# Retention of a head pair, four tiles at a time, in a hybrid attention, convolution and retention layer

## The chip, the cores and the metric

The kernel runs on one core of a Trainium2 chip. The metric is the device time of one execution in microseconds (us), as the median of several runs. In the rows PE is TensorE (matrix products and transposes), PEld its loading of the stationary operand, DVE is VectorE, ACT is ScalarE, POOL is GpSimd and SP issues the transfers.

## The reference

One layer over 2048 tokens of width 1024. The normalised input goes through one projection whose columns feed three mixers: chunked softmax attention (6 heads of 64), a convolution module, and retention (6 heads of 64). Their outputs meet in one output projection with a residual; a squared-ReLU feed-forward of width 4096 and a gated embedding follow. The part that matters here is the retention, cut to its core:

```python
intra = einsum(einsum(qc, kc) * d_intra, vc)          # inside a chunk, with decay
kv    = einsum(k_dec, vc)                             # 64 x 64 per chunk and head
prev  = scan: state = chunk_decay * state + kv        # state before each chunk
cross = einsum(q_dec, prev)
out   = intra + cross
out   = (out - mean) * rsqrt(var + EPS) * gn_g        # per head
return silu(g) * out
```

## The kernel before, in words

Tokens are worked on in four blocks of 512 (`T`), each of four tiles of 128 tokens (`NT`). A block goes through the projections, mixers, output projection, feed-forward and gate. Large products are done as three fp32r matmuls (high and low parts); transposes and the small products of attention and retention are plain fp32, and the trace shows such a small product as two instructions.

Heads are taken in three pairs. For each pair `att_proj` (L371) and `ret_proj` (L508) make the projections; `ret_proj` leaves per tile a buffer `rn` of 512 columns: q, k (both rotated), v and the gate. The copies out of PSUM for a tile end in two POOL additions and multiplications (L535 finishes q and k, L540 the gate). `rn` tiles come from a pool of four.

`ret_mix` (L546) does the retention of a pair tile by tile, in a loop over the four tiles. Each tile has one PSUM bank `s` from `rbank` (L110), a pool of a single bank, so the next tile's first transpose needs the release of this tile's bank. In the bank the loop puts the transposes of q and k, the scores of both heads, the key-value product and the output. Between the PE steps ACT copies k (L557) and q (L561), DVE writes q once more into `qz` with zeros in the other head's rows (L560), DVE multiplies the scores by the decay mask (L566), ACT copies the output (L575), DVE updates the running state of both heads (L578), and a group norm follows: statistics (L582, L583), epsilon (L585), power -0.5 on POOL (`rstd`, L181 and L182), subtraction of the mean on DVE (L589), two POOL multiplications (L591, L592). After the last tile four transposes (`roT`) bring the output into the layout of the output projection, and `split_tr` (L184) writes its high and low parts.

The order of PE's instructions is written out: every matmul and transpose keeps its program order. `trunk` walks through the large products as segments; after each of their matmuls `advance` (L801) may insert steps of two chains that run beside them, chain 0 the attention of a pair (`att_mix`, L401), chain 1 the retention and the convolution's end (`conv_mix`, L325). A step is a generator's stretch between two `yield`s. The value that is yielded (from the table `W`, L234) is how long PE is to do other work before the chain's next step, measured on a model clock `clk` that grows with each PE instruction by a fixed cost (L48 to L56):

```python
if t[1] > pos and clk[0] < t[4]:   # L816: not yet, unless past its deadline
    break
...
t[4] = clk[0] + d + 0.01           # L822: earliest clock of the next step
```

Retention of pair 0 and 1 may start at a fifth of the next `att_proj`, that of pair 2 at 3% of the output projection's first part (`wo_a`), and has its deadline near the end of the next `ret_proj`, or at the start of `wo_b`. The order on the other engines is the scheduler's.

Of the kernel before, what the change touches and what calls it, by code (L numbers as in the profile page):

```python
# [12 lines left out]
F32R = mybir.dt.float32r  # L13
AF = mybir.ActivationFunctionType
ALU = mybir.AluOpType
AX = mybir.AxisListType

P = 128
D = 1024
S = 2048  # L20
T = 512
NB = S // T
NT = T // P
KT = D // P
HD = 64
# [15 lines left out]
def trunk(ctx, tc, a, out):  # L41
    nc = tc.nc
    V, A, G = nc.vector, nc.scalar, nc.gpsimd
    clk, posn = [0.0], [0.0]

    class PE:
        @staticmethod
        def matmul(o, x, y, start, stop):  # L48
            n = y.shape[-1]
            clk[0] += max(n, 256) / 2400.0 if y.dtype == F32R else max(4 * n, 512) / 2400.0  # L50
            tc.keep_in_program_order(nc.tensor.matmul(o, x, y, start=start, stop=stop))  # L51

        @staticmethod
        def transpose(o, x, i):
            clk[0] += 256 / 2400.0
            tc.keep_in_program_order(nc.tensor.transpose(o, x, i))  # L56

    cpool = ctx.enter_context(tc.tile_pool(name="const", bufs=1))
# [3 lines left out]
    def ctile(name, shape, src=None, dt=F32):  # L62
        t = cpool.tile(shape, dt, tag=name, name=name)
        if src is not None:
            nc.sync.dma_start(t, src)
        return t

    def stile(tag, bufs, shape, name=None, dt=F32):
        return sp.tile(list(shape), dt, tag=tag, name=name or tag, bufs=bufs)
# [40 lines left out]
    def rbank(name):  # L110
        return ps.tile([P, 512], F32, tag="r", name=name, bufs=1)
# [4 lines left out]
    def f(t):  # L116
        return t.bitcast(F32)
# [63 lines left out]
    def rstd(o, var, n):  # L181
        G.tensor_tensor(o, var, nhalf[:, :n], ALU.pow)  # L182

    def split_tr(b, hi, lo, scale):  # L184
        A.activation(hi, b, AF.Copy, scale=scale)
        V.scalar_tensor_tensor(lo, b, scale, f(hi), ALU.mult, ALU.subtract)
# [44 lines left out]
        A.activation(r, b[:, :T], AF.Copy)  # L231

    cur = {}
    W = dict(qk=0.7, qs=2.5, st=5.2, ss=1.2, ts=2.4, vo=1.6, r1=2.6, r2=1.6, r3=1.5, r4=4, c1=3.5, c2=2.6, c3=0.6)  # L234

    def xnorm(blk):
        xh, xl = big("xh", 0), big("xl", 1)
# [87 lines left out]
    def conv_mix():  # L325
# [3 lines left out]
        for u in range(2):  # L329
# [13 lines left out]
            for i in range(2):  # L343
                V.tensor_scalar(z[u][:, i * DC : i * DC + DC], b2[:, i], s6[:, 12 + 2 * i : 13 + 2 * i],
                                s6[:, 18 + i : 19 + i], ALU.subtract, ALU.mult)
            yield W["c1"]
        hl = []
        for c in range(2):
# [7 lines left out]
            hl.append((yh, yl))  # L356
            yield W["c2"]
        yield W["c3"]
        for c in range(2):
# [8 lines left out]
            V.scalar_tensor_tensor(ml[:, c], b, bias, f(mh[:, c]), ALU.add, ALU.subtract)  # L368
            yield W["c2"]

# [25 lines left out]
    def mix():  # L396
        if "m" not in cur:
            cur["m"] = big("mh", 2), big("ml", 3)
        return cur["m"]

    def att_mix(p):  # L401
# [6 lines left out]
        for j, gain in enumerate((qg, kg)):  # L408
# [3 lines left out]
            for h in range(2):  # L412
# [5 lines left out]
                if j == 0:  # L418
                    A.activation(q[h][y], b[x], AF.Copy, scale=gain[x, 0:1])
            yield W["qk"]  # L420
        yield W["qs"]
        rs = stile("rs", 2, [P, 16])
# [121 lines left out]
        yield from gemm(range(NT), KT, 5, tok(xh, xl), lambda t, k: rhs(k), 512, evac)  # L544

    def ret_mix(p):  # L546
        nats = cur["rn", p]
        o = stile("ro", 1, [P, NT, P])
        for t in range(NT):
            n = nats[t]  # L550
            s = rbank("rs")
            for j in range(2):
                PE.transpose(s[:, j * P : j * P + P], n[:, j * P : j * P + P], ident)
            kT = stile("rk", 1, [P, P])
            at = stile("rat", 1, [P, 256])
            qT = stile("rq", 1, [P, P])
            A.activation(kT, s[:, P:256], AF.Copy)  # L557
            for h in range(2):
                hr = slice(h * HD, h * HD + HD)
                V.tensor_copy(qz[hr, h], s[hr, :P])  # L560
            A.activation(qT, s[:, :P], AF.Copy)  # L561
            yield W["r1"]
            PE.matmul(s[:, 256:], kT, qz.rearrange("p h n -> p (h n)"), start=True, stop=True)
            yield 0
            PE.matmul(s[:, P:256], n[:, P : 2 * P], n[:, 256:384], start=True, stop=True)
            V.tensor_tensor(at, s[:, 256:], rmask[:, 2 * p : 2 * p + 2].rearrange("p h n -> p (h n)"), ALU.mult)  # L566
            yield W["r2"]
            PE.matmul(s[:, :P], qT, st[p], start=True, stop=False)
            yield 0
            for h in range(2):  # L570
                hr = slice(h * HD, h * HD + HD)
                PE.matmul(s[:, hr], at[:, h * P : h * P + P], n[:, 256 + h * HD : 256 + h * HD + HD],
                          start=False, stop=(h == 1))
                yield 0
            A.activation(o[:, t], s[:, :P], AF.Copy)  # L575
            for h in range(2):
                hr = slice(h * HD, h * HD + HD)
                V.scalar_tensor_tensor(st[p][hr, hr], st[p][hr, hr], gstate[hr, p : p + 1],  # L578
                                       s[hr, P + h * HD : P + h * HD + HD], ALU.mult, ALU.add)
            g6 = stile("g6", 2, [P, 20])  # L580
            for h in range(2):
                V.bn_stats(g6[:, 6 * h : 6 * h + 6], o[:, t, h * HD : h * HD + HD])  # L582
                V.bn_aggr(g6[:, 12 + 2 * h : 14 + 2 * h], g6[:, 6 * h : 6 * h + 6])  # L583
            gv = g6[:, 12:16].rearrange("p (h c) -> p h c", c=2)[:, :, 1]
            V.tensor_tensor(g6[:, 16:18], gv, geps[:, 2 * p : 2 * p + 2], ALU.add)  # L585
            rstd(g6[:, 18:20], g6[:, 16:18], 2)
            for h in range(2):
                hr = slice(h * HD, h * HD + HD)
                V.tensor_scalar(o[:, t, hr], o[:, t, hr], g6[:, 12 + 2 * h : 13 + 2 * h], None, ALU.subtract)  # L589
            o3 = o[:, t].rearrange("p (h d) -> p h d", d=HD)  # L590
            G.tensor_tensor(o3, o3, g6[:, 18:20].unsqueeze(2).to_broadcast([P, 2, HD]), ALU.mult)  # L591
            G.tensor_tensor(o[:, t], o[:, t], n[:, 384:], ALU.mult)  # L592
            yield W["r3"]
        yield W["r4"]
        mh, ml = mix()
        b = rbank("roT")
        for t in range(NT):
            PE.transpose(b[:, t * P : t * P + P], o[:, t], ident)
        split_tr(b, mh[:, RT[p]], ml[:, RT[p]], gng[:, p : p + 1])
        yield 0  # L600

# [133 lines left out]
    segs, start = [], {}  # L735
# [46 lines left out]
    for b in range(NB):  # L782
        if b:
            place(lambda b=b: xnorm(b), spread(13, at(("g2", b - 1, 6), 0.05), at(("g2", b - 1, 7), 0.95)))
            place(late, spread(8, at(("conv", b), 0.01), at(("conv", b), LE)))
            place(lambda b=b: ple_load(b - 1), [at(("conv", b), 0.3)])
            place(late_rstd, [at(("conv", b), LF), at(("conv", b), LF + 0.15)])
        if b:
            chain(1, conv_mix, at(("ap", b, 0), CS), at(("ap", b, 1), CE))
        for p in range(NPAIR):  # L790
            nxt = ("rp", b, p + 1) if p < 2 else ("wob", b)
            chain(0, lambda p=p: att_mix(p), at(("rp", b, p), AS if b or p else AS0), at(nxt, 0.0))
            chain(1, lambda p=p: ret_mix(p), at(("ap", b, p + 1), RS) if p < 2 else at(("woa", b), RT0),
                  at(nxt, RE if p < 2 else 0.0))
            if b == 0 and p == 0:
                chain(1, conv_mix, at(("ap", b, 1), CS0), at(("rp", b, 2), CE0))
        place(norm2, [at(("g1", b, 0), NE), at(("g1", b, 0), NF)])
# [26 lines left out]
                    c.pop(0)  # L824

    with tc.high_priority(offset=AHEAD):
        nhalf = ctile("nhalf", [P, 4])
        G.memset(nhalf, -0.5)
        ng = ctile("ng", [P, 3, KT])
        ident = ctile("ident", [P, P])  # L830
        make_identity(nc, ident)
        ones = ctile("ones", [P, 1])
        A.activation(ones, nhalf[:, 0:1], AF.Copy, scale=-2.0)
        kdec = ctile("kdec", [P, NH], a["kdec"])
# [5 lines left out]
    for c in range(2):  # L840
        with tc.high_priority(offset=AHEAD):
            next(first)
        x = slice(c * HALF, c * HALF + HALF)
# [18 lines left out]
    rmask = ctile("rmask", [P, NH, P], a["rmask"])  # L862
    geps = ctile("geps", [P, NH], a["geps"])
    gstate = ctile("gstate", [P, NPAIR], a["gstate"])
    hist = ctile("hist", [P, 2, NTAP - 1])
    G.memset(hist, 0.0)
    qz = ctile("qz", [P, 2, P])
    G.memset(qz, 0.0)
    st = []
    for p in range(NPAIR):  # L870
        st.append(ctile(f"st{p}", [P, P]))
        G.memset(st[p], 0.0)

    pos = 0.0
    for gen in segs:
# [92 lines left out]
```

## Time and profile before

| | |
|---|---|
| Median of three runs | 2852.79 us (2850.76 to 2854.25) |
| Span of the profiled execution | 2853.1 us, 0.3 us over the median of the runs |
| PE busy | 2777.3 us, 97% |
| DVE, ACT, POOL busy | 1580.2, 1126.5, 1121.1 us (55%, 39%, 39%) |
| Retention per execution | 12 times `ret_mix` (4 blocks, 3 pairs), 48 tiles |

The page's shares are averages over stages. The timeline gives for a group of instructions its start, its length, and in brackets how long its engine was idle before it and what ended that. The groups by line and shape give busy time, the mean length of one, and the idle time before with its causes. Start to start of neighbouring matmuls is what one costs PE, since their lengths overlap.

### The profile page before, as it was taken

The page shows a single profiled execution, that of the slowest core. Times are in us where ns is not written, and L with a number is a line of the kernel's source. Part 1 is how long each engine was busy: PE and PEld are TensorE (multiplying, and loading weights), DVE is VectorE, ACT ScalarE, POOL GpSimd, SP SyncE. Part 2 cuts the span into 40 slices and gives each one's busy share as a digit, 9 for nine tenths or more (in the row PEclk, how much of TensorE's full clock was granted, in tenths as well). Part 3 has the DMA queues.
Part 4 walks back from the last instruction along what each step waited for, and adds up shares of the span by engine and source line. Part 5 has one row for each costly group of instructions (what it writes and reads, how often), then busy time and mean ns, then how long its engine had stood idle before and what let it go on. Part 6 is the DMA issues. An engine that isn't in the chain of part 4 may idle for free. (4 is left out here: it accounts for less than half of the span.)

```text
span 2853.1 us, 36805 instructions
## 1 busy us (share of the span) xinstructions
PE 2777.3 (97%) x13178; PEld 2233.5 (78%) x13178; DVE 1580.2 (55%) x2811; ACT 1126.5 (39%) x2210; POOL 1121.1 (39%) x1038
## 2 busy tenths in 40 slices
PE   7999999999999999999999999999999999999999
PEld 6777788887788778888778877888877877788887
DVE  6966433348766653334876664333487666433343
ACT  4554322243455432224345543222434554322333
POOL 4434433335444343333544434333354443433333
PEclk9999999999999999999999999999999999999999
DMA  5123222242212322224221232222422122222221
GB/s 179 62 85 115 94 90 95 96 140 88 85 62 75 123 96 90 96 96 138 90 85 62 74 124 96 90 95 96 140 87 85 62 97 82 89 93 93 96 103 67
DMA packets 89030, 271.80 MB, mean 95 GB/s; under 512 B 11024, under 2 KB 11792, under 8 KB 88848
## 3 DMA queue, kind: packets, MB, share of 16 engines
q1 hardware_dynamic: 88848, 269.45, 27.4%
q8 instruction: 105, 1.72, 0.2%
q14 instruction: 77, 0.63, 0.1%
HBM read 261.02 MB, written 8.39 MB: 94 GB/s over the span
## 5 line engine op out<-in xcount | busy, mean ns | idle before, releaser
L123 POOL TENSOR_TENSOR w<-raw,w 128x512 fp32r<-128x512 f32 (+1 forms) x439 | 584.4, 1333 | 1163.8 <-ACT w L122 826.7
L122 ACT ACTIVATE w<-raw 128x512 fp32r<-128x512 f32 (+1 forms) x880 | 536.5, 618 | 1109.5 <-PE acc L51 630.6
L51 PE MATMUL acc<-xh,w 128*128 128x512 f32 (+1 forms) x1744 | 563.9, 396 | 0.0
L51 PE MATMUL acc<-w,xh 128*128 128x512 f32 (+1 forms) x1536 | 489.8, 384 | 3.1 <-DVE w L123 1.9
L123 DVE TENSOR_TENSOR w<-raw,w 128x512 fp32r<-128x512 f32 (+1 forms) x441 | 337.4, 767 | 155.8 <-ACT w L122 140.0
L51 PEld LDWEIGHTS acc<-xh,w 128*128 128x128 f32 x1744 | 328.8, 189 | 77.9
L51 PE MATMUL acc<-hid,w 128*128 128x512 f32 x1536 | 373.3, 395 | 0.0
L51 PE MATMUL w<-hid,w 128*128 128x512 f32 x1536 | 368.8, 395 | 0.0
L51 PE MATMUL acc<-xl,w 128*128 128x512 f32 (+1 forms) x872 | 345.9, 397 | 8.7 <-DVE xl L207 8.7
L51 PEld LDWEIGHTS w<-hid,w 128*128 128x128 f32 x1536 | 287.9, 187 | 70.5
L51 PEld LDWEIGHTS acc<-hid,w 128*128 128x128 f32 x1536 | 287.9, 187 | 70.3
L51 PE MATMUL w<-xh,w 128*128 128x512 f32 x1024 | 328.3, 396 | 0.0
L51 PEld LDWEIGHTS acc<-w,xh 128*128 128x128 f32 x1536 | 283.1, 189 | 43.2 <-issue 7.8
L51 PE MATMUL acc<-w,xl 128*128 128x384 f32 (+1 forms) x768 | 293.0, 382 | 0.0
L655 DVE TENSOR_TENSOR hid<-s,hid 128x512 fp32r<-128x512 f32 x128 | 91.9, 718 | 280.6 <-POOL s L653 280.6
L313 DVE SCALAR_TENSOR_TENSOR y<-gl,cw,y 128x512 f32<-128x512 f32 x240 | 235.4, 1006 | 2.2
L51 PEld LDWEIGHTS w<-xh,w 128*128 128x128 f32 x1024 | 192.0, 188 | 47.0
L51 PEld LDWEIGHTS acc<-xl,w 128*128 128x128 f32 x872 | 165.1, 189 | 52.8 <-DVE xl L207 14.7
L51 PE MATMUL w<-xl,w 128*128 128x512 f32 x512 | 202.1, 395 | 0.0
L679 DVE TENSOR_TENSOR h<-h,w 128x512 f32<-128x512 f32 x128 | 87.9, 686 | 178.5 <-PE w L51 178.5
L679 DVE TENSOR_TENSOR h<-h,acc 128x512 f32<-128x512 f32 x128 | 87.4, 685 | 139.9 <-PE acc L51 139.8
L51 PEld LDWEIGHTS acc<-w,xl 128*128 128x128 f32 x768 | 145.5, 189 | 16.4 <-issue 3.3
(173 smaller groups left out, 3495.3 us busy)
## 6 DMA issues: line engine op xcount, KB each, us to landing
raw<-in_w_dram SPq DMA_DIRECT2D x256, 512.0 KB, 3.4
raw<-in_wr_dram SPq DMA_DIRECT2D x48, 512.0 KB, 3.5
raw<-in_w_g_dram SPq DMA_DIRECT2D x40, 512.0 KB, 3.4
raw<-in_wa_dram SPq DMA_DIRECT2D x48, 384.0 KB, 3.0
raw<-in_w_oa_dram SPq DMA_DIRECT2D x24, 512.0 KB, 3.4
xraw<-in_xT_dram SPq DMA_DIRECT2D x32, 256.0 KB, 4.1
xs<-in_x_dram SPq DMA_DIRECT2D x32, 256.0 KB, 3.9
h<-in_xT_dram SPq DMA_DIRECT2D x32, 256.0 KB, 4.4
```

The lines of the kernel that those rows point to most:

```text
L51: tc.keep_in_program_order(nc.tensor.matmul(o, x, y, start=start, stop=stop))
L122: A.activation(w[:, 0, :n], x, AF.Copy)
L123: eng.tensor_tensor(w[:, 1, :n], x, f(w[:, 0, :n]), ALU.subtract)
L313: V.scalar_tensor_tensor(y, gl[:, j : j + T], cw[:, c, j : j + 1], y, ALU.mult, ALU.add)
L655: V.tensor_tensor(hid[:, 4 + j], s, f(hid[:, j]), ALU.subtract)
L679: V.tensor_tensor(h[j], h[j], b, ALU.add)
```

## The change

Retention is done stage by stage over the four tiles. First come the four key-value products in one bank (`rkv`), and from it the eight state updates, into separate buffers: the state before each tile is kept (`now`, three `stm`, `nxt`). Then the four transposes of q (`rqT`), those of k (`rkT`), the scores of two tiles at a time (`rsc`, twice), and one bank (`rout`) for the cross and value products of all tiles, copied out by one instruction. The group norm's epsilon, power, subtraction and first multiplication run once over four tiles, the statistics still once per tile and head, the gate multiplication once per tile. The waits of the chain become r0 = 1.0 after the state updates, r1 = 2.0 after each set of transposes, r2 = 1.6 after each pair of scores and r3 = 7 before `roT`; before they were 2.6, 1.6 and 1.5 per tile and 4 at the end. The model clock gets new costs, which hold for the attention and the convolution chain too. Buffers grow (`qz`, `rq`, `rk`, `rat`, `g6`, `nhalf`), and the scratch kept for dynamic DMA is set to 1024 bytes.

```diff
             n = y.shape[-1]
-            clk[0] += max(n, 256) / 2400.0 if y.dtype == F32R else max(4 * n, 512) / 2400.0
+            if y.dtype == F32R:
+                clk[0] += max(n, 240) / 2200.0
+            else:
+                clk[0] += max(4 * n * x.shape[-1] / P, 240) / 2200.0
...
-            clk[0] += 256 / 2400.0
+            clk[0] += 240 / 2200.0
...
-    W = dict(qk=0.7, qs=2.5, st=5.2, ss=1.2, ts=2.4, vo=1.6, r1=2.6, r2=1.6, r3=1.5, r4=4, c1=3.5, c2=2.6, c3=0.6)
+    W = dict(qk=0.7, qs=2.5, st=5.2, ss=1.2, ts=2.4, vo=1.6, r0=1.0, r1=2.0, r2=1.6, r3=7, c1=3.5, c2=2.6, c3=0.6)
...
+        ns = cur["rn", p]
+        hrs = slice(0, HD), slice(HD, P)
+        now, nxt = st[p]
+        st[p].reverse()
+        b = rbank("rkv")
+        for t in range(NT):
+            PE.matmul(b[:, t * P : t * P + P], ns[t][:, P : 2 * P], ns[t][:, 256:384], start=True, stop=True)
+        states = [now] + stm + [nxt]
+        for t in range(NT):
+            for hr in hrs:
+                V.scalar_tensor_tensor(states[t + 1][hr, hr], states[t][hr, hr], gstate[hr, p : p + 1],
+                                       b[hr, t * P + hr.start : t * P + hr.stop], ALU.mult, ALU.add)
+        yield W["r0"]
+        b = rbank("rqT")
+        for t in range(NT):
+            PE.transpose(b[:, t * P : t * P + P], ns[t][:, :P], ident)
+        qT = stile("rq", 1, [P, T])
+        for h, hr in enumerate(hrs):
+            V.tensor_copy(qz[hr, :, h], b[hr].rearrange("p (t n) -> p t n", n=P))
+        A.activation(qT, b, AF.Copy)
+        yield W["r1"]
+        b = rbank("rkT")
+        for t in range(NT):
+            PE.transpose(b[:, t * P : t * P + P], ns[t][:, P : 2 * P], ident)
+        kT = stile("rk", 1, [P, T])
+        A.activation(kT, b, AF.Copy)
+        yield W["r1"]
...
+        for u in range(2):
+            b = rbank("rsc")
+            for i in range(2):
+                t = 2 * u + i
+                PE.matmul(b[:, i * 256 : i * 256 + 256], kT[:, t * P : t * P + P],
+                          qz[:, t].rearrange("p h n -> p (h n)"), start=True, stop=True)
+            V.tensor_tensor(at[:, 2 * u : 2 * u + 2], b.rearrange("p (t n) -> p t n", n=256), mask, ALU.mult)
+            yield W["r2"]
+        b = rbank("rout")
+        for t in range(NT):
+            PE.matmul(b[:, t * P : t * P + P], qT[:, t * P : t * P + P], states[t], start=True, stop=False)
             for h in range(2):
...
+                PE.matmul(b[:, t * P + h * HD : t * P + h * HD + HD], at[:, t, h * P : h * P + P],
+                          ns[t][:, 256 + h * HD : 256 + h * HD + HD], start=False, stop=(h == 1))
+        o = stile("ro", 1, [P, T])
+        A.activation(o, b, AF.Copy)
...
+        for g in range(8):
+            V.bn_stats(g6[:, 6 * g : 6 * g + 6], o[:, g * HD : g * HD + HD])
+            V.bn_aggr(g6[:, 48 + 2 * g : 50 + 2 * g], g6[:, 6 * g : 6 * g + 6])
...
+        rstd(g6[:, 72:80], g6[:, 64:72], 8)
+        o3 = o.rearrange("p (g d) -> p g d", d=HD)
+        V.tensor_tensor(o3, o3, mv[:, :, 0].unsqueeze(2).to_broadcast([P, 8, HD]), ALU.subtract)
+        G.tensor_tensor(o3, o3, g6[:, 72:80].unsqueeze(2).to_broadcast([P, 8, HD]), ALU.mult)
+        for t in range(NT):
+            x = slice(t * P, t * P + P)
+            G.tensor_tensor(o[:, x], o[:, x], ns[t][:, 384:], ALU.mult)
+        yield W["r3"]
```

## Rows read from the trace of the kernel before

**Rows 1.** The page: busy time per engine, and DVE's in 40 slices

```profile
PE 2777.3 (97%) x13178; PEld 2233.5 (78%) x13178; DVE 1580.2 (55%) x2811; ACT 1126.5 (39%) x2210; POOL 1121.1 (39%) x1038
...
DVE  6966433348766653334876664333487666433343
```

**Rows 2.** Windows of block 2: its mixers, its feed-forward (length, busy us, clock)

```profile
1457.00:1706.00 249.00, 245.81 (x1407) 199.79 (x1406) 157.86 (x376) 127.13 (x292) 101.45 (x120) 1.00 0.25 84
1712.00:2080.00 368.00, 365.83 (x1575) 293.36 (x1574) 150.27 (x217) 127.03 (x211) 134.68 (x110) 1.00 0.30 103
```

**Rows 3.** Groups by shape: PE in the retention, with idle time before

```profile
L51 PE MATMUL rs<-qz,rk 128*128 128x256 f32 x96 | 31.5, 409 | 6.3 <-ACT rq L561 6.3
...
L56 PE MATMUL rs<-ident,rn 128*128 128x128 f32 x96 | 18.6, 275 | 7.3 <-DVE st L578 6.7 <-ACT w L122 0.3
```

**Rows 4.** Groups by shape: DVE and ACT in the retention

```profile
L560 DVE COPY qz<-rs 64x128 f32<-64x128 f32 x96 | 27.4, 285 | 8.4 <-ACT rk L557 6.2
L578 DVE SCALAR_TENSOR_TENSOR st<-st,gstate,rs 64x64 f32<-64x64 f32 x96 | 26.6, 277 | 34.1 <-ACT ro L575 33.0
...
L566 DVE TENSOR_TENSOR rat<-rs,rmask 128x256 f32<-128x256 f32 x48 | 20.2, 422 | 40.2 <-PE rs L51 40.0
...
L582 DVE BATCH_NORM_STATS2 g<-ro 128x6 f32<-128x64 f32 x96 | 16.4, 213 | 1.1
...
L583 DVE BATCH_NORM_AGGREGATE g<-g 128x2 f32<-128x6 f32 x96 | 15.2, 176 | 0.0
...
L561 ACT ACTIVATE rq<-rs 128x128 f32<-128x128 f32 x48 | 13.3, 276 | 32.0 <-DVE qz L560 31.5
```

**Rows 5.** Groups by shape: the nearest to the change's new shapes

```profile
L182 POOL TENSOR_TENSOR ass<-ass,nhalf 128x4 f32<-128x4 f32 x48 | 52.8, 1101 | 128.2 <-DVE ass L387 126.7
...
L182 POOL TENSOR_TENSOR g<-g,nhalf 128x2 f32<-128x2 f32 x48 | 33.7, 702 | 63.0 <-DVE g L585 62.9
...
L389 POOL TENSOR_TENSOR an<-qk,ass 128x256 f32<-128x256 f32 x48 | 31.3, 652 | 3.8
...
L591 POOL TENSOR_TENSOR ro<-ro,g 128x128 f32<-128x128 f32 x48 | 23.5, 489 | 3.7
...
L231 ACT ACTIVATE r<-rb 128x512 f32<-128x512 f32 x8 | 4.8, 598 | 5.8 <-PE rb L56 5.8
...
L459 DVE COPY pT<-sc 128x512 f32<-128x512 f32 x3 | 2.1, 693 | 0.1
```

**Rows 6.** Timeline of PE, block 2: value products, and a tile's first transposes

```profile
1616.73 0.48 PE L51 MATMUL acc<-w,xh 128*128 128x512 f32 x1
1617.05 0.33 PE L51 MATMUL rs<-rn,rat 128*128 128x64 f32 x2
1617.18 0.48 PE L51 MATMUL acc<-w,xh 128*128 128x512 f32 x1
1617.50 0.40 PE L51 MATMUL acc<-w,xl 128*128 128x512 f32 x1
1617.73 0.63 PE L51 MATMUL acc<-w,xh 128*128 128x512 f32 x2
...
1620.73 0.41 PE L56 MATMUL rs<-ident,rn 128*128 128x128 f32 x2 [1.20 <-DVE st L578]
```

**Rows 7.** Timeline of PE, block 2: the pair's last value product, its final transposes

```profile
1628.10 0.33 PE L51 MATMUL rs<-rn,rat 128*128 128x64 f32 x2
...
1636.19 0.60 PE L56 MATMUL roT<-ident,ro 128*128 128x128 f32 x4
1636.54 0.48 PE L51 MATMUL acc<-w,xh 128*128 128x512 f32 x1
```

**Rows 8.** Timeline of POOL: the last multiplication of the same pair

```profile
1634.54 0.46 POOL L592 TENSOR_TENSOR ro<-ro,rn 128x128 f32<-128x128 f32 x1
```

**Rows 9.** Timeline of PE, block 3: the third pair's first transposes

```profile
2366.56 0.38 PE L56 MATMUL rs<-ident,rn 128*128 128x128 f32 x2
```

**Rows 10.** Timeline of POOL, block 3: q and k of that pair's last tile finished

```profile
2367.07 0.74 POOL L535 TENSOR_TENSOR rn<-rn,rb 128x256 f32<-128x256 f32 x1 [0.83 <-DVE rn L533]
```

More of the change, by code (lines that the diff above doesn't have):

```diff
@@ L546, in ret_mix @@
     def ret_mix(p):
-        nats = cur["rn", p]
-        o = stile("ro", 1, [P, NT, P])
-        for t in range(NT):
[L550 to L557, printed above, removed]
-            for h in range(2):
[L559 to L593, printed above, removed]
@@ L594, in ret_mix @@
-        yield W["r4"]
+        ns = cur["rn", p]
[3 more added lines that the diff above has]
+        b = rbank("rkv")
+        for t in range(NT):
+            PE.matmul(b[:, t * P : t * P + P], ns[t][:, P : 2 * P], ns[t][:, 256:384], start=True, stop=True)
[4 more added lines that the diff above has]
+                                       b[hr, t * P + hr.start : t * P + hr.stop], ALU.mult, ALU.add)
@@ new lines, in ret_mix @@
+        kT = stile("rk", 1, [P, T])
+        A.activation(kT, b, AF.Copy)
+        yield W["r1"]
+        at = stile("rat", 1, [P, NT, 2 * P])
+        mask = rmask[:, 2 * p : 2 * p + 2].rearrange("p h n -> p (h n)").unsqueeze(1).to_broadcast([P, 2, 2 * P])
+        for u in range(2):
[6 more added lines that the diff above has]
+            yield W["r2"]
@@ new lines, in ret_mix @@
+        b = rbank("rout")
+        for t in range(NT):
+            PE.matmul(b[:, t * P : t * P + P], qT[:, t * P : t * P + P], states[t], start=True, stop=False)
+            for h in range(2):
+                PE.matmul(b[:, t * P + h * HD : t * P + h * HD + HD], at[:, t, h * P : h * P + P],
+                          ns[t][:, 256 + h * HD : 256 + h * HD + HD], start=False, stop=(h == 1))
+        o = stile("ro", 1, [P, T])
+        A.activation(o, b, AF.Copy)
+        g6 = stile("g6", 1, [P, 80])
@@ new lines, in ret_mix @@
+        mv = g6[:, 48:64].rearrange("p (g c) -> p g c", c=2)
+        for g in range(8):
+            V.bn_stats(g6[:, 6 * g : 6 * g + 6], o[:, g * HD : g * HD + HD])
+            V.bn_aggr(g6[:, 48 + 2 * g : 50 + 2 * g], g6[:, 6 * g : 6 * g + 6])
+        V.tensor_tensor(g6[:, 64:72].rearrange("p (t h) -> p t h", h=2), mv[:, :, 1].rearrange("p (t h) -> p t h", h=2),
+                        geps[:, 2 * p : 2 * p + 2].unsqueeze(1).to_broadcast([P, NT, 2]), ALU.add)
+        rstd(g6[:, 72:80], g6[:, 64:72], 8)
@@ L597, in ret_mix @@
         for t in range(NT):
-            PE.transpose(b[:, t * P : t * P + P], o[:, t], ident)
+            PE.transpose(b[:, t * P : t * P + P], o[:, t * P : t * P + P], ident)
         split_tr(b, mh[:, RT[p]], ml[:, RT[p]], gng[:, p : p + 1])
@@ L826, in trunk @@
     with tc.high_priority(offset=AHEAD):
-        nhalf = ctile("nhalf", [P, 4])
+        nhalf = ctile("nhalf", [P, 8])
         G.memset(nhalf, -0.5)
@@ L866, in trunk @@
     G.memset(hist, 0.0)
-    qz = ctile("qz", [P, 2, P])
+    qz = ctile("qz", [P, NT, 2, P])
     G.memset(qz, 0.0)
@@ L870, in trunk @@
     for p in range(NPAIR):
-        st.append(ctile(f"st{p}", [P, P]))
-        G.memset(st[p], 0.0)
+        st.append([ctile(f"st{p}{i}", [P, P]) for i in range(2)])
+        for x in st[p]:
+            G.memset(x, 0.0)
+    stm = [ctile(f"stm{i}", [P, P]) for i in range(NT - 1)]
+    for x in stm:
+        G.memset(x, 0.0)
     pos = 0.0
@@ L955 @@
     from concourse.bass_utils import run_bass_kernel_spmd as _run
-    nc = _bacc.Bacc("TRN2", target_bir_lowering=False, num_devices=1)
+    nc = _bacc.Bacc("TRN2", target_bir_lowering=False, num_devices=1, dynamic_dma_scratch_size=1024)
     arrays, aps = {}, {}
```

## The prediction

> **What bounds the kernel.** I read the page's busy times first: PE is busy for 2777.3 of 2853.1 us, and no other engine comes near [rows 1]. [...] So the time is PE's row of instructions, one after the other, and a change in retention counts only through PE: how many instructions it has, what each costs, and how long it stands at one whose input is late. DVE is not full in the mixers (157.9 of 249.0 us), though in the first block two slices are at 9 [rows 1, 2].
>
> The groups of retention's PE instructions then show the waits. PE stood 7.3 us before a tile's first transposes, almost all for DVE's state update, which holds the only bank, and 6.3 us before the scores, for ACT's copy of q [rows 3]. That copy waits in turn for DVE's copy of q, and the state update waits for ACT's copy of the output, though these read other columns [rows 4]: here two engines are never let into one bank together, and a bank is handed on only when its last reader is done. Fourteen microseconds, 0.5%, is what shorter waits can give at most by these rows.
>
> **The change part by part.** The profiled span is the base of the sum. It lies 0.3 us over the median of the runs, which I ignore. Any difference under 0.2% (5.7 us) counts as none, as that is about what a measurement of this kernel can tell.
>
> *PE's own work.* Per pair there are as many transposes (12) and small products (20) as before. Only grouping can save. A value product that stands alone costs 1617.50 - 1616.73 = 0.77 us less two large matmuls of 0.23 us (the step from 1617.50 to 1617.73), so 0.30 us [rows 6]. In a group, four transposes move the next large matmul by 1636.54 - 1636.19 = 0.35 us, 0.09 us a pass [rows 7], and a product has two passes: about 0.2 us at best. Eight products in 12 pairs give 96 x 0.1 = 10 us; some already stand beside attention's products, and the last of each group still pays, so I take -5 us, between 0 and -10.
>
> *The old waits.* The 13.6 us of [rows 3] go away as such. Part of them belongs to the first block, where DVE stays full [rows 1]. I take -12 us, between 0 and -14.
>
> *DVE, ACT, POOL.* Eight copies of 285 ns become two of 64x512 at about 693 ns, eight mean subtractions become one, and so on [rows 4, 5]. That is tens of microseconds of engine time over the run, but none of it on PE. I count nothing for it; the cover is PE's large matmuls, which run on beside it except where PE waits for the last of a stage. That case is what follows.
>
> *First new wait, r0.* The transposes of q need the bank of the key-value products, so all eight state updates must be done. Need: 0.28 us until the last product has landed (a small one's length [rows 3]), then 8 x 0.277 = 2.2 us [rows 4], together 2.5 us without any queue. Cover: r0 = 1.0 on the new clock, where a 512-column matmul counts 512/2200 = 0.233, just its measured step [rows 6]. So five large matmuls, 1.2 us, and 0.1 us of the product itself. That leaves 1.2 us uncovered. DVE's queue adds to the need (it is 63% busy in the mixers), attention's products add to the cover. I take 1.7 us, 12 times, +20 us. Ends: 0.6 us if updates start before the last product (+7), 2.2 us with a queue (+26). DVE's other work queues behind the eight updates for as long; attention's next transposes are the first to feel it, and their wait of 5.2 covers it (if not, up to 1 us a pair).
>
> *Second new wait, r1 after q.* Need: 0.28 + 2 x 0.69 (copies of 512 columns) + 0.60 (ACT's copy of as many, after DVE's) = 2.3 us [rows 4, 5], and some 0.5 us of queue. Cover 2.0, with overshoot 2.4 us. I take 0.3 us, +4 us, between 0 and +12. After k there is one ACT copy (0.9 us in all, cover 2.0), and after the scores one DVE product of 512 columns (422 ns for 256 [rows 4], so about 0.7; 1.1 us in all, cover 1.6): nothing.
>
> *Third new wait, r3.* From the last value product to `roT`: 0.3 until it lands; ACT copy 0.60; sixteen statistics, whose starts I put 0.12 us apart as DVE overlaps such short ones (their lengths add to 3.1 us [rows 4]), so 1.9 to 3.1; epsilon 0.2; power on POOL, 702 ns for two columns and 1101 for four, so 0.2 a column and 1.9 us for eight; broadcast multiplication, 489 at 128 columns and 652 at 256, so 1.0 at 512; four gate multiplications of 0.46 [rows 5, 8], 1.9 us. With hand-overs 8.0 us at the least. The subtraction runs beside the power. What queues add is seen in the old tail: last value product at 1628.10, last POOL multiplication over at 1635.00, so 6.9 us [rows 7, 8], where the lengths alone make about 3.8. So some 2 to 3 us more, and a need of 10 to 11 us. Cover: 7.0, which attention stretches. The old 5.5 on the old clock took 1636.19 - 1628.10 = 8.1 us [rows 7], of which large matmuls alone would make 6.0. I take 8.7 us. That leaves 1.7 us, 12 times, +20 us; ends 0 and 3.5 us (+42). POOL's weight splits queue behind 4.8 us of this; they run far ahead of PE.
>
> *Start of a pair.* Before, the first step needed only the first tile's `rn`; now the fourth product needs the last tile's k. In the third pair that is finished at 2367.81, 1.25 us after the first step [rows 9, 10]; three products of 0.2 us pass meanwhile, so 0.6 us a block, more in the first block with its full DVE. Take +4 us, 0 to +10.
>
> *The clock.* For attention and convolution a wait now spans 8% fewer large matmuls (0.213 against 0.233 each), while attention's value products count for about half. Both signs, so 0, within 5 us either way. The scratch and the buffer sizes: 0, since all transfers of the loops are SP's.
>
> Sum: 2853 - 5 - 12 + 20 + 4 + 20 + 4 = 2884 us.
>
> [...]
>
> **The rivals.**
>
> *Faster.* The new waits are mostly covered. It decides at the third wait: if attention's products stretch r3 to the 10 us that the tail needs, and r0 costs its 0.6, the sum is 2853 - 17 + 7 = 2843 us; with the full -24, 2836. For it: 5.5 became 8.1 in [rows 7], so 7 may well become 9 or 10; fewer DVE instructions shorten queues, most in the first block. Against it: the 2.2 us of updates behind a wait of 1.0 need no queue to be late. Chance 0.22. [...]
>
> *A wash.* Two of the three waits are covered, or all at half their size: 2853 - 17 + 20 = 2856 us, within 5.7 us of before. Chance 0.11.
>
> *The first block decides.* DVE there is at 9 in two slices [rows 1], with convolution work of 1 us a piece; if it gets between eight updates or sixteen statistics, each of three pairs stands 5 us longer in two places: 2884 + 30 = 2914 us. It is the upper part of my slower case.
>
> *The change doesn't do what it says.* If the chain met its deadlines, steps would follow without spacing and every stage would show in full. A pair's waits add to 15.2 on the clock against 8.1 for the old tail alone [rows 7], so the chain ends sooner than before, and I give it 0.01, slower.
>
> **How the numbers follow.** Slower, my forecast with its worse variants: 0.67; within 0.2%: 0.11; faster: 0.22. The slower case's own range is 2859 to 2930. Adding the favourable ends of all parts gives 2836, the unfavourable ones 2943; a tenth left out on each side gives 2840 to 2926.
>
> **What would show it.** Right: PE idle before the transposes of q, for DVE's state update, 1 to 2 us in nearly every pair; idle before `roT`, for POOL's last multiplication; a small wait before the fourth key-value product in third pairs; no wait before the scores. Wrong: `roT` without idle time, which would move 20 us; or idle before `rqT` under 0.5 us, which would mean that DVE begins with the first product or that attention's work fills r0. Waits of attention's transposes that grow by more than 5 us would say that the new clock matters by itself.

## The result and the profile after

The changed kernel took 2952.14 us as the median of four runs (2946.87 to 2957.3), against 2852.85 us before: ratio 1.0349, 95% interval 1.0334 to 1.0363, so 99 us slower. The direction was the forecast one; the size was not, for the range ended at 2926.

The profiled execution has a span of 2945.0 us, 91.9 more than before. Below, first the busy times and DVE's slices from its page, to be set beside [rows 1].

```profile
PE 2823.2 (96%) x13178; PEld 2260.4 (77%) x13178; DVE 1529.0 (52%) x2595; ACT 1114.3 (38%) x2102; POOL 1100.9 (37%) x972
...
DVE  7855533348755453334875455333487555533343
```

PE has as many instructions as before, 13178, and DVE, ACT and POOL each have less to do: the busy time that was to be saved was saved (DVE 51 us, and its one slice at 9 is gone), and bought nothing. But PE was busy for 45.9 us more, and idle for 2945.0 - 2823.2 = 121.8 us where it had been idle for 2853.1 - 2777.3 = 75.8. So half of the loss is 46.0 us of new idle time, and half is PE being busy for longer with as many instructions. Most of the latter goes with the mean granted clock:

```profile
core 0: 2945.0 us, clock 0.982
```

Before it was 0.995. My estimate of what the clock takes from a run, out of the two figures of this view, is (1 - mean clock) x span: 0.018 x 2945.0 = 53.0 us now and 0.005 x 2853.1 = 14.3 us before, so some 39 us more (each within 1.5 us, as the clock is given to 0.001). That leaves 91.9 - 46.0 - 38.7 = 7 us, of which more below.

Where the new idle time is, the groups by shape say (columns as in [rows 3]: busy, mean ns, then idle time before and what ended it). First two rows of the kernel before, then those of the changed kernel, whose L54 and L59 are L51 and L56 of the kernel before:

```profile
L51 PE MATMUL acc<-w,xh 128*128 128x512 f32 x768 | 273.6, 418 | 3.0 <-DVE w L123 1.9 <-ACT v L383 0.9 <-ACT rn L527 0.2
...
L56 PE MATMUL roT<-ident,ro 128*128 128x128 f32 x48 | 7.2, 272 | 0.0
```

```profile
L54 PE MATMUL acc<-w,xh 128*128 128x512 f32 x768 | 270.0, 419 | 16.0 <-ACT rn L530 12.9 <-DVE w L126 2.0 <-ACT v L386 0.9
...
L59 PE MATMUL roT<-ident,ro 128*128 128x128 f32 x48 | 16.0, 332 | 16.8 <-POOL ro L608 14.3
...
L54 PE MATMUL rkv<-rn 128*128 128x128 f32 x96 | 14.3, 286 | 3.6 <-POOL rn L538 3.6
...
L59 PE MATMUL rqT<-ident,rn 128*128 128x128 f32 x48 | 8.4, 304 | 17.6 <-DVE st L560 17.6
L59 PE MATMUL rkT<-ident,rn 128*128 128x128 f32 x48 | 8.4, 302 | 0.5 <-ACT rq L569 0.3
```

The 13.6 us of [rows 3] are gone. In their place stand 17.6 us before `rqT`, 16.8 before `roT`, 3.6 before the key-value products and 0.5 before `rkT`. One row is not retention's at all: the large matmuls of 512 columns, which had 3.0 us of idle time before, now have 16.0, of which 12.9 for ACT's copy of the gate into `rn` (L530, in `ret_proj`). These rows make -13.6 + 38.5 + 13.0 = +37.9 of the 46.0 us; the rest lies in small rows of the convolution and the attention.

The row of `roT` holds more waiting than its idle time says, for its busy time went from 7.2 to 16.0 us. Each of the four transposes now waits for its own tile's POOL multiplication. The page gives a transpose a length of 0.33 us, and a wait that falls inside such a length counts as busy. In the timeline below the group moves the next matmul by 1598.96 - 1597.59 = 1.37 us, against 0.35 in [rows 7]. Over the twelve groups of the trace these steps add to 17.8 us against 4.3 before; 5.0 of them are counted as idle. So 8.5 us of waiting stand in PE's busy time, about as much as the 7 us that are left over above. That they are the same is not shown.

And this is how a piece of idle time goes on to cost more than itself. PE's timeline in block 2, at one `roT` and at one wait for the gate:

```profile
1597.59 1.71 PE L59 MATMUL roT<-ident,ro 128*128 128x128 f32 x4 [1.57 <-POOL ro L608]
1598.96 0.67 PE L54 MATMUL acc<-w,xl 128*128 128x384 f32 x1
1599.43 0.84 PE L54 MATMUL acc<-w,xh 128*128 128x384 f32 x2
1600.07 0.52 PE L54 MATMUL acc<-w,xl 128*128 128x384 f32 x1
1600.39 0.84 PE L54 MATMUL acc<-w,xh 128*128 128x384 f32 x2
...
1615.43 0.50 PE L54 MATMUL acc<-w,xh 128*128 128x512 f32 x1 [1.74 <-ACT rn L530]
```

The windows around them (length, busy time of PE, PEld, DVE, ACT, POOL, granted clock, DMA share, GB/s); the first is the block's mixers as in [rows 2]:

```profile
1505.80:1754.60 248.80, 235.04 (x1314) 188.37 (x1314) 136.12 (x311) 117.97 (x255) 90.55 (x98) 0.97 0.23 74
1598.90:1602.30 3.40, 3.40 (x12) 3.40 (x13) 2.24 (x3) 2.47 (x4) 2.68 (x3) 0.50 0.33 103
1602.30:1615.90 13.60, 11.86 (x56) 9.33 (x55) 6.01 (x12) 7.64 (x16) 6.52 (x7) 1.00 0.21 63
1615.90:1626.20 10.30, 10.30 (x24) 6.71 (x23) 3.22 (x9) 2.87 (x8) 0.45 (x1) 0.50 0.00 0
```

In the mixers PE is now idle for 13.8 us of 248.8 (before 3.2 of 249.0), at a mean clock of 0.97 (before 1.00). Right behind `roT`, for 3.4 us, the clock is at 0.50; behind the wait for the gate it is there for 10.3 us. There, three matmuls of 384 columns take 1600.39 - 1599.43 = 0.96 us; further on in the timeline, at full clock (1602.30 to 1602.82), three take 0.52.

### The profile page after: what moved, and what is told of

The parts are those of the page before. It is cut to its first block, busy times and chain, and to the rows that moved or that the text cites. A ratio compares the mean times of both kernels' runs of the same rounds, so it can differ in the third digit from the quotient of the medians.

```text
span 2945.0 us, 36267 instructions
## 1 busy us (share of the span) xinstructions
PE 2823.2 (96%) x13178; PEld 2260.4 (77%) x13178; DVE 1529.0 (52%) x2595; ACT 1114.3 (38%) x2102; POOL 1100.9 (37%) x972
## 5 line engine op out<-in xcount | busy, mean ns | idle before, releaser
L54 PE MATMUL acc<-xh,w 128*128 128x512 f32 (+1 forms) x1744 | 564.9, 396 | 0.0
L54 PE MATMUL acc<-w,xh 128*128 128x512 f32 (+1 forms) x1536 | 487.1, 388 | 16.9 <-ACT rn L530 12.9
L54 PEld LDWEIGHTS acc<-xh,w 128*128 128x128 f32 x1744 | 329.0, 189 | 78.0
L54 PE MATMUL acc<-hid,w 128*128 128x512 f32 x1536 | 374.7, 396 | 0.0
L54 PE MATMUL w<-hid,w 128*128 128x512 f32 x1536 | 370.2, 396 | 0.0
L54 PE MATMUL acc<-xl,w 128*128 128x512 f32 (+1 forms) x872 | 344.8, 395 | 8.7 <-DVE xl L210 8.7
L54 PEld LDWEIGHTS w<-hid,w 128*128 128x128 f32 x1536 | 289.2, 188 | 70.8
L54 PEld LDWEIGHTS acc<-hid,w 128*128 128x128 f32 x1536 | 289.3, 188 | 69.9
L54 PEld LDWEIGHTS acc<-w,xh 128*128 128x128 f32 x1536 | 289.5, 194 | 63.7 <-ACT rn L530 16.6
L54 PE MATMUL w<-xh,w 128*128 128x512 f32 x1024 | 329.4, 397 | 0.0
L54 PE MATMUL acc<-w,xl 128*128 128x384 f32 (+1 forms) x768 | 297.3, 387 | 0.0
L670 DVE TENSOR_TENSOR hid<-s,hid 128x512 fp32r<-128x512 f32 x128 | 91.9, 718 | 280.5 <-POOL s L668 280.5
L54 PEld LDWEIGHTS w<-xh,w 128*128 128x128 f32 x1024 | 191.9, 188 | 46.7
L54 PEld LDWEIGHTS acc<-xl,w 128*128 128x128 f32 x872 | 165.0, 189 | 53.0 <-DVE xl L210 14.9
L54 PE MATMUL w<-xl,w 128*128 128x512 f32 x512 | 200.8, 392 | 0.0
L54 PEld LDWEIGHTS acc<-w,xl 128*128 128x128 f32 x768 | 149.6, 195 | 21.0 <-issue 5.5
```

The source lines that it names most:

```text
L670: V.tensor_tensor(hid[:, 4 + j], s, f(hid[:, j]), ALU.subtract)
```

## The experiments

My theory was that the loss is the three new waits and what the granted clock takes after them; the rivals were the new costs of the model clock, and that grouped small products lower the clock by themselves. All kernels compute the whole output. Beside each time stand the ratio to the kernel before on the same chip and its interval.

**The model clock, undone and alone.** e1 is the changed kernel with the old costs, e2 the kernel before with the new ones; the diff is that of e1, which e2 reverses.

```diff
-            if y.dtype == F32R:
-                clk[0] += max(n, 240) / 2200.0
-            else:
-                clk[0] += max(4 * n * x.shape[-1] / P, 240) / 2200.0
+            clk[0] += max(n, 256) / 2400.0 if y.dtype == F32R else max(4 * n, 512) / 2400.0
...
-            clk[0] += 240 / 2200.0
+            clk[0] += 256 / 2400.0
```

> The changed kernel with the model clock's old costs. Theory (three new PE waits, and the slower granted clock that follows them): the waits in the chain become 9% longer in large matmuls, so the idle time before rqT and roT shrinks a little; 2930 to 2950 us against 2952. Rival (the new clock itself shifted attention's and convolution's steps to bad places): 2890 us or less.

> The kernel before with only the model clock's new costs. Theory: 2848 to 2862 us, PE idle before retention's steps much as before. Rival (the new clock is the loss): 2885 us or more, with PE idle before attention's transposes or before large matmuls that wait for ACT.

e1: 2924.65 us, 1.0251 (1.0236 to 1.0267). e2: 2872.83 us, 1.0069 (1.0054 to 1.0084). Both lie between what theory and rival wanted, so neither was right: the new costs cost 20 us on the kernel before, and 27 us come back when the changed kernel loses them, so they are a part of the loss of their own, and the grouping is the larger part. In e2 the old wait before the scores grew while the one before the transposes went from 7.3 us [rows 3] to under one:

```profile
L54 PE MATMUL rs<-qz,rk 128*128 128x256 f32 x96 | 32.0, 416 | 11.3 <-ACT rq L564 11.2
...
L59 PE MATMUL rs<-ident,rn 128*128 128x128 f32 x96 | 18.4, 273 | 0.7 <-DVE st L581 0.6
```

**One wait at a time.** e3 gives the final transposes more time (the value in the table `W`); e4 frees the bank of the key-value products early, by a copy on ACT from which DVE makes the state updates.

```diff
-r3=7
+r3=12
```

```diff
+        kvs = stile("rkvs", 1, [P, T])
+        A.activation(kvs, b, AF.Copy)
...
-                                       b[hr, t * P + hr.start : t * P + hr.stop], ALU.mult, ALU.add)
+                                       kvs[hr, t * P + hr.start : t * P + hr.stop], ALU.mult, ALU.add)
```

> The changed kernel with r3 = 12 in place of 7. Theory: the idle time before roT (16.8 us) goes, and with it the half-clock stretches that follow it; 2915 to 2935 us. Rival (the new clock): 2945 us or more, since roT's wait would only move elsewhere.

> The changed kernel, but ACT copies the four key-value products into SBUF and DVE updates the states from there, so that the bank is free after one copy. Theory: idle before rqT falls from 17.6 to under 5 us and half-clock stretches after it go; 2905 to 2935 us. Rival (the new clock, or DVE's queue as such): 2945 us or more.

e3: 2929.53 us, 1.0267 (1.025 to 1.0284). e4: 2933.77 us, 1.0281 (1.0266 to 1.0296). Each is within its expectation by the time, but the rows say that the idle time as a whole hardly changed (117.3 and 122.4 us, from 121.8): it moved. In e3 the wait before `roT` is gone, and attention's transposes `qkT`, at 4.2 us in the changed kernel, wait longer for POOL's `an`:

```profile
L59 PE MATMUL qkT<-ident,an 128*128 128x128 f32 x96 | 17.2, 289 | 11.7 <-POOL an L392 11.7
...
L59 PE MATMUL roT<-ident,ro 128*128 128x128 f32 x48 | 7.5, 274 | 0.2 <-POOL ro L608 0.2
```

In e4 the transposes of q no longer wait, and those of k take over, since in e4's text ACT's copy of q stands behind DVE's copies into `qz`, and these behind the state updates (in the trace of the changed kernel the last updates start at 1652.25, the copies at 1653.66, and ACT's at 1655.33):

```profile
L59 PE MATMUL rkT<-ident,rn 128*128 128x128 f32 x48 | 7.9, 287 | 16.2 <-ACT rq L571 16.2
L59 PE MATMUL rqT<-ident,rn 128*128 128x128 f32 x48 | 7.8, 286 | 0.1
```

What both gained (23 and 18 us by the medians) is more in the clock (0.985 and 0.986, from 0.982) than in idle time.

**All waits long.** e5 lengthens the three waits to what the trace had shown to be needed, with the old model clock; e7 does it with the new one. The diff shows the values in `W`.

```diff
-r0=1.0, r1=2.0, r2=1.6, r3=7
+r0=3.4, r1=3.0, r2=1.6, r3=11
```

> The changed kernel with the old clock costs and long waits: r0 = 3.4, r1 = 3.0, r3 = 11. Theory (the loss is PE idle at too short waits, and the half clock that follows idle): idle before rqT, rkT and roT under 4 us in all, half-clock time down from 109 to 50 us or less, 2850 to 2875 us; what is left is the wait before the fourth key-value product and large matmuls that wait for ACT. Rival (grouping itself is slow: dense small products lower the clock, or the bursts block DVE and POOL): 2895 us or more, with half-clock time still above 70 us though PE has no such idle.

> The changed kernel as it is, new clock, with the same long waits. Theory: as with the old clock but for the new clock's own cost, some 20 us by the run that changed it alone: 2870 to 2895 us. Rival (the clock's costs matter only through the short waits): within 5 us of the run with the old clock.

e5: 2907.4 us, 1.0199 (1.018 to 1.0219). e7: 2899.66 us, 1.0166 (1.0149 to 1.0183). In e5 the waits before `rqT`, `rkT` and `roT` are under 1 us together (the one before the key-value products rose to 7.7), and 54 us of the loss remained: my theory was not complete. The time lies where the rival put it, and the half of the rival that speaks of bursts shows in the rows below. Its other half does not: what the clock takes is 0.009 x 2905.8 = 26 us, so the half clock stood for some 52 us, not for more than 70. The rows of e5:

```profile
L51 PE MATMUL acc<-w,xh 128*128 128x512 f32 x768 | 268.4, 419 | 29.5 <-POOL w L123 13.6 <-ACT rn L527 12.9 <-DVE w L123 1.9
...
L56 PE MATMUL qkT<-ident,an 128*128 128x128 f32 x96 | 16.7, 284 | 10.5 <-POOL an L389 10.5
...
L56 PE MATMUL roT<-ident,ro 128*128 128x128 f32 x48 | 8.5, 292 | 0.3 <-POOL ro L605 0.2
...
L56 PE MATMUL rqT<-ident,rn 128*128 128x128 f32 x48 | 7.4, 277 | 0.5 <-DVE st L557 0.5
```

The large matmuls now stand 29.5 us, 13.6 of them for POOL's split of the weights (L123), and `qkT` 10.5 us. POOL's group norm comes in one burst now, which the kernel before had in twelve small pieces per pair. In the changed kernel, POOL's timeline before one `roT`:

```profile
1593.01 1.63 POOL L185 TENSOR_TENSOR g<-g,nhalf 128x8 f32<-128x8 f32 x1
1594.61 0.61 POOL L392 TENSOR_TENSOR an<-qk,ass 128x256 f32<-128x256 f32 x1
1595.19 1.49 POOL L605 TENSOR_TENSOR ro<-ro,g 128x512 f32<-128x512 f32 x1
1596.76 2.02 POOL L608 TENSOR_TENSOR ro<-ro,rn 128x128 f32<-128x128 f32 x4
1598.74 1.27 POOL L126 TENSOR_TENSOR w<-raw,w 128x512 fp32r<-128x512 f32 x1
```

Attention's `an` and the weight split stand between and behind its pieces. In e7 neither expectation came true: it is 8 us faster than e5, not slower or equal. Its idle time is 99.5 us, against 112.4 in e5, and lies elsewhere: 24.7 us before `qkT`, 6.0 for POOL's split and 2.4 for ACT's copy of the gate.

That leaves the 12.9 us for ACT's copy of the gate, the same in the changed kernel and in e5, and 15.5 in e1, so it does not come from the new model clock. The order on ACT there is (changed kernel, a second place of the same block):

```profile
1691.32 0.46 ACT L526 ACTIVATE rqk<-acc,xss 128x256 f32<-128x256 f32 x1
1691.80 0.68 ACT L422 ACTIVATE q<-qkT,qg 64x512 fp32r<-64x512 f32 x1
1692.49 0.31 ACT L529 ACTIVATE rn<-acc,xss 128x64 f32<-128x64 f32 x1
1692.84 0.68 ACT L418 ACTIVATE k<-qkT,kg 64x512 fp32r<-64x512 f32 x1
1693.54 0.32 ACT L529 ACTIVATE rn<-acc,xss 128x64 f32<-128x64 f32 x1
1693.76 0.36 ACT L530 ACTIVATE rn<-acc,xss 128x128 f32<-128x128 f32 x1
```

and PE meets it with nothing in hand:

```profile
1692.04 0.39 PE L54 MATMUL acc<-w,xl 128*128 128x512 f32 x1
1694.17 0.50 PE L54 MATMUL acc<-w,xh 128*128 128x512 f32 x1 [1.74 <-ACT rn L530]
```

In the kernel before, ACT has the same six copies in the same order (1626.98 to 1629.79), but PE has other work in that time, products of retention and then four of attention:

```profile
1627.65 0.33 PE L51 MATMUL rs<-rn,rat 128*128 128x64 f32 x2
...
1628.10 0.33 PE L51 MATMUL rs<-rn,rat 128*128 128x64 f32 x2
...
1628.79 0.22 PE L51 MATMUL sc<-k,q 128*128 128x128 f32 x1
1628.93 0.32 PE L51 MATMUL sc<-k,ql 64*128 64x128 f32 x1
1629.19 0.50 PE L51 MATMUL sc<-k,q 128*128 128x512 f32 x1
1629.62 0.49 PE L51 MATMUL sc<-k,ql 64*128 64x512 f32 x1
1630.04 0.50 PE L51 MATMUL acc<-w,xh 128*128 128x512 f32 x1
```

The large matmul comes at 1630.04, when the copy is done, without idle time. In the changed kernel attention's four products come right behind that large matmul (from 1694.50) and not before it. So small steps had been cover here for the copy of a gate that they neither write nor read; the change moved their places in PE's row, also those of attention's steps, which it did not edit.

**Cover put back.** e6 is e5 with the third pair's retention (RT0) and the attention (AS) started later; e8 also lets attention's deadline lie later. e9 gives attention's new start and deadline (not RT0) to the kernel before, and e10 is e8 with the new model clock. Of the line that sets the starts, the diff shows the two values.

```diff
-AS=0.25, RT0=0.03
+AS=0.42, RT0=0.12
...
-            chain(0, lambda p=p: att_mix(p), at(("rp", b, p), AS if b or p else AS0), at(nxt, 0.0))
+            chain(0, lambda p=p: att_mix(p), at(("rp", b, p), AS if b or p else AS0), at(nxt, 0.38 if p < 2 else 0.0))
```

> As the run before, and the third pair's retention starts at 12% of the output projection's first part instead of 3%, attention at 42% of its retention projection instead of 25%. Theory: the wait before the fourth key-value product (8 us) and the wait of large matmuls for ACT's copies in the retention projections (about 2 us in six of them) go as well; 2835 to 2860 us. Rival: attention that starts later meets its deadline and its steps come without spacing, 2870 us or more.

> The run with old clock, long waits and later starts, and attention's deadline moved from the start of the next retention projection to 38% of it. Theory (each loss is one late hand-over to PE, and can be taken away singly): the 15 us idle before the transposes rT go, 2836 to 2856 us. Rival (the bursts on DVE and POOL that grouping makes only push the idle time to another place): 2860 us or more, with idle time before other instructions of PE up by as much.

> The kernel before, tile by tile, with attention's later start and later deadline alone. Theory: its waits in retention stay (13 us), 2845 to 2862 us. Rival (what the run above gains comes from attention's place and not from grouped retention): as fast as that run or faster, 2845 us or less.

> As the first of these three, with the new clock costs. Theory (the new clock costs time by itself, as in the two pairs measured so far by +20 and -8 us, so it only moves steps): within 15 us of that run, either way. Rival (the new clock, set to the measured rate of large matmuls, is the better one once waits are long): 10 us or more below it.

e6: 2866.08 us, 1.0043 (1.0028 to 1.0058), between theory and rival. The large matmuls' idle time fell from 29.5 to 3.3 us and that before the key-value products from 7.7 to 0.8, and a new wait of 15.3 us came up in attention, as the rival said:

```profile
L51 PE MATMUL acc<-w,xh 128*128 128x512 f32 x768 | 258.6, 408 | 3.3 <-DVE w L123 1.9 <-POOL w L123 0.6 <-ACT v L383 0.5
...
L56 PE MATMUL rT<-ident,rb 128*128 128x128 f32 x48 | 9.1, 321 | 15.3 <-DVE rb L490 15.3
```

e8: 2854.85 us (11 runs), 1.0005 (0.9996 to 1.0014): with the later deadline that wait is 2.4 us, as the theory said, and the grouped retention is as fast as the kernel before. Its span and clock, PE's busy time and the large matmuls:

```profile
core 0: 2854.1 us, clock 0.995
...
PE 2777.3 (97%) x13178; PEld 2236.1 (78%) x13178; DVE 1539.0 (54%) x2595; ACT 1112.2 (39%) x2104; POOL 1107.5 (39%) x972
...
L51 PE MATMUL acc<-w,xh 128*128 128x512 f32 x768 | 259.8, 408 | 7.5 <-POOL w L123 5.1 <-DVE w L123 1.9 <-ACT v L383 0.3
```

Clock and busy time are those of the kernel before, the idle time is 76.8 us, and the wait for the gate is gone. All of retention's small products are grouped here, so grouped products do not lower the clock by themselves: that rival falls.

e9: 2863.63 us, 1.0034 (1.0021 to 1.0046), 1.6 us over its expectation. So attention's place alone does not do it; with attention there, per tile is 9 us slower than grouped, though its waits and RT0 were not set anew for it. e10: 2869.75 us, 1.0057 (1.0044 to 1.007): the new model clock costs 15 us here too, at the edge of the expectation. In e7 it had been 8 us better than the old one, so its price hangs on the waits around it, and it has no fixed sign.

**POOL's burst shortened.** e11 is e8 with the broadcast multiplication of the norm on DVE.

```diff
-        G.tensor_tensor(o3, o3, g6[:, 72:80].unsqueeze(2).to_broadcast([P, 8, HD]), ALU.mult)
+        V.tensor_tensor(o3, o3, g6[:, 72:80].unsqueeze(2).to_broadcast([P, 8, HD]), ALU.mult)
```

> The run with old clock, long waits, later starts and later deadline, and the broadcast multiplication of the group norm on DVE instead of POOL. Theory (what is left against the kernel before is POOL's burst, which delays the split of weights, 1.55 us before a large matmul in each block): that idle time goes, 2843 to 2853 us. Rival (DVE becomes the late one): 2856 us or more.

2853.41 us (11 runs), 1.0002 (0.9994 to 1.0011): 0.4 us over the expectation, and not to be told from the kernel before, nor from e8. The large matmuls' wait for POOL's split went from 5.1 to 2.9 us and not to nothing. No version tried beats it.

**The control without any grouping.** e12 is the kernel before with one wait taken from the tile loop, so that retention runs closer together.

```diff
-r3=1.5
+r3=0.0
```

> The kernel before, tile by tile, with the wait between tiles r3 = 0 instead of 1.5, so that PE comes too early to each tile's first transposes. Theory (idle time before retention costs its own length and, where the granted clock falls after it, more): idle there up from 7 us by 25 to 45 us, half-clock time up by 20 us or more, and the span up by clearly more than the idle time. Rival (the clock has nothing to do with these waits; it fell in the changed kernel for its grouped small products): half-clock time within 7 us of before, span up by the idle time alone.

2896.29 us, 1.0145 (1.013 to 1.0161): 43 us lost with the old stage order, the old model clock and no grouped product. Its rows, and a window:

```profile
L51 PE MATMUL acc<-w,xh 128*128 128x512 f32 x768 | 272.4, 422 | 7.4 <-ACT rn L527 4.3 <-DVE w L123 1.9 <-ACT v L383 0.7
...
L56 PE MATMUL rs<-ident,rn 128*128 128x128 f32 x96 | 19.6, 287 | 28.9 <-DVE st L578 23.7 <-ACT w L122 3.3 <-POOL ass L182 1.9
```

```profile
862.60:872.80 10.20, 10.20 (x22) 6.68 (x22) 4.05 (x10) 3.12 (x9) 0.46 (x1) 0.50 0.00 1
```

The wait before the transposes grew by 21.6 us over [rows 3] (25 were expected at least), the wait for the gate appeared (4.3 us, from 0.2 before), and the window, at half clock, begins 862.60 - 861.85 = 0.75 us behind one of them (1.54 us, ending at 861.85). Idle time rose by 104.8 - 75.8 = 29.0 us and what the clock takes by 0.009 x 2900.3 - 14.3 = 12 us. The profiled execution is 47 us longer than that of the kernel before, so some 6 us are left without a name here too. Lost cover and the half clock behind a stall come without grouped products as well, which agrees with e8 on the rival that these lower the clock.

## Why the prediction was right in direction and wrong in size

- **The three new waits** came for the causes that were named. r0: predicted 20 us, measured 17.6 before `rqT`, for DVE's state update, from 0.4 to 2.4 us a pair. r3: predicted 20, measured 16.8 of idle time before and in `roT`, for POOL's multiplications, and 25 with the 8.5 us that its row counts as busy. In block 2, from the start of a pair's last two value products (1588.15) to the end of POOL's last multiplication (1598.78), the tail took 10.6 us, so the need of 10 to 11 was right; the cover was 1597.59 - 1.57 - 1588.15 = 7.9 us, where I had 8.7. r1: 4, measured 0.5. The start of a pair: 4, measured 3.6. No wait came before the scores, as said.
- **The single durations** held: power for eight columns 1930 ns (1.9 us), `qz` 689 ns (693), mask 691 ns (0.7 us), ACT's copies 591 and 598 ns (0.60); only the broadcast multiplication was 1213 ns for 1.0 us.
- **The old waits** went in full: 13.6 for 12. **PE's own work**: -5 was forecast and is not to be seen; e8, at the same clock, has PE busy for 2777.3 us as before.
- These wait terms make +36 in the sum (-12 + 20 + 4 + 20 + 4), and +24.9 by the rows. Had they been all, the time would have been near 2878, or near 2886 with the 8.5 us inside `roT`. What failed is what the sum left out:
- **"I count nothing for it; the cover is PE's large matmuls, which run on beside it"**, in the part on DVE, ACT and POOL. PE's row is one written order, and the large matmuls wait for these engines too. 13.0 us of new idle time stand before them in the changed kernel, and 8 more in small rows. I priced the steps that the change moves by what they cost and not by what they covered; e6 and e8 took the wait for the gate away by moving attention's steps and the third pair's. "They run far ahead of PE", of the weight splits, held in the changed kernel, but not once r3 was long: 13.6 us in e5. The burst that I put at 4.8 us takes 1598.78 - 1593.01 = 5.8 in the timeline above, with `an` inside.
- **Idle time was priced at its own length.** The step is the sum itself, which has no term for the granted clock. Some 39 us of the 92 are that. The window of [rows 2] showed the mixers at 1.00, and I took this for granted in a kernel whose waits I was about to raise.
- **"The clock"** (the model's): 0 within 5 us. Measured, 20 us alone (e2), 27 us back (e1), 15 us in e10, and a gain of 8 in e7. The balance of signs that I argued did not bound the size; the new costs move every step of three chains against work whose timing they don't know. These differences overlap with the two points above and are not added to them. The 5 us each way were left out of the ends 2836 and 2943, which with them are 2831 and 2948.
- **The rivals.** The faster one fell, since neither r0 nor r3 was covered. The first block did not decide either: from the end of one block's last gate product to the next one's, the four blocks are 20.6, 27.9, 23.4 and 19.9 us longer than before. [rows 1] also has one slice of DVE at 9 in that block, not the two that the prediction read. Fewer and larger instructions did not shorten the span: the changed kernel has 2595 instructions on DVE for 2811, DVE is 52% busy, and PE is idle for 121.8 us in place of 75.8; e8 has 2595 as well, with 76.8 us of idle time and the time of the kernel before. The subtraction of the mean went from 33.0 us (96 instructions of 64 columns, L589) to 8.2 (12 of 512, L604, by another operation). That is half of the 51 us that DVE lost in busy time, and the span did not hang on DVE's busy time.

Open stay whether the 7 us are the 8.5 inside `roT` (e3, where nothing waits there, still lacks 74.8 - 41.5 - 29.6 = 3.7 us); how e5 to e8 divide between the later start of the third pair and that of the attention, which were always moved together; and why the new model clock helped in e7 and hurt elsewhere.

## What to carry to other kernels

Before small steps on a full engine are gathered into stages, ask what each of them covers where it stands now, other chains' hand-overs included, and space the stages by the whole of their hand-over (here 3.4 and 11 us, not 1 and 7). A wait that is lengthened alone moves its idle time to the next hand-over (in e3 the 16.8 us before `roT` became 0.2, and the idle time of the span 117.3 of 121.8), so judge such an edit by the idle time of the whole span and the mean granted clock, not by the row that it mends. Price a new stall of TensorE at more than its length: here 46.0 us of new idle time came with an estimated 39 us that the clock took.

## What the hardware showed that was not expected

One stall of 1.57 us, with the slow transposes right behind it, was followed by 3.4 us at half clock, one of 1.74 us by 10.3 us, with PE working throughout the slow stretch, as the windows above show. Not every stall was: the 1.20 us in [rows 6] lies in the mixers of block 2 before, whose clock was 1.00 throughout [rows 2]. Counted over PE's timeline from 30 us on, the changed kernel has 33 idle pieces of over 1.3 us, and after 18 of them a stretch at half clock began within 6 us (the bounds are mine, for the count); the kernel before has 13, and 5 of them were so followed. Of pieces between 0.15 and 0.8 us, 4 of 33 and none of 24 were. The amount of idle time does not settle it: e5 was idle for 112.4 us and e1 for 116.3, and the clock took, by the estimate from its mean, 0.009 x 2905.8 = 26 us from the one and 0.013 x 2922.1 = 38 us from the other. What else decides, these runs don't tell.
